# A macaron decoder layer on one core: three more tiles of the second feed-forward in the wide form, and the decay vectors made behind another head

## The chip, the cores and the metric

The kernel runs on one core of a Trainium2 chip. The metric is device time in microseconds (us) for one execution, the median of several runs. The core has a matrix engine (PE, whose weight loads are shown apart as PEld), a vector engine (DVE), a scalar engine (ACT), GpSimd (POOL) and a sync engine (SP) that here only issues DMAs. Each engine works through its own list of instructions strictly in order, and engines wait for each other by semaphores. Matmul results land in PSUM, which has eight banks of 128 partitions x 512 fp32 values; everything else lies in SBUF.

## The reference

One decoder layer over 512 tokens of width 1024, all fp32:

```python
f = swiglu(rms_norm(h, ffn1_norm_pre), ffn1_w_gate, ffn1_w_up, ffn1_w_down)
h = h + 0.5 * rms_norm(f, ffn1_norm_post)
u = rms_norm(h, mix_norm_pre)
q, k, v, xr, yr, gl = split(u @ w_in)          # 12 heads of 128; 1024; 1024; 2 x 1024
attn = 3 groups of 4 heads, dilated sliding windows, merged by log-sum-exp
xc = width-4 causal convolution of xr
log_a = -8 * sigmoid(gate_a) * softplus(-a_param)      # RG-LRU, a recurrence over time
rec = scan(exp(log_a), ...) * gelu(yr)
merged = sigmoid(gl)[0] * (attn @ w_attn) + sigmoid(gl)[1] * (rec @ w_rec)
h = h + rms_norm(merged @ w_out, mix_norm_post)
f = swiglu(rms_norm(h, ffn2_norm_pre), ffn2_w_gate, ffn2_w_up, ffn2_w_down)
h = h + 0.5 * rms_norm(f, ffn2_norm_post)
```

where `swiglu(x) = (silu(x @ w_gate) * (x @ w_up)) @ w_down` with a hidden width of 2816, which is 22 tiles of 128.

## The kernel before, in words

**fp32 products from three.** An fp32 operand is split into a high part (ACT copies it into the matrix engine's fp32r type, line 303) and a low part (DVE subtracts, line 304). A product is then three matmuls: high x high, high x low, low x high. Every weight goes through such a split on the chip: SP fetches 512 KB into one of four `raw` slots (line 243), ACT and DVE split it into one of four `w8` tiles, and only when the low part is done is the `raw` slot free for the next fetch.

**Seven products instead of eight.** Most pairs of weight tiles go through one level of Strassen's method in Winograd's form. For hidden tile `f` of a feed-forward, the weights of up (`u0`, `u1`) and gate (`g0`, `g1`) are fetched, four sums of them are made on DVE, and all seven forms are split (`w_forms`, lines 685 to 703: four additions at lines 692, 693, 694 and 697, then three splits of 1024 columns and one of 512). The products p1 to p7, each over four blocks of k, then make 128 x 512 results of gate and up. The forms of tile f+1 are made while tile f is on PE.

There are two ways to do the seven products.

- `seven_on` (the narrow form, matmuls at lines 730 to 732): each result is 256 columns wide, each block of k takes three matmuls of 256 columns, 84 matmuls in all. Four half banks of PSUM are used. Results on the way are copied by ACT alone (line 744, four copies of 256 columns); DVE adds at lines 970 and 975 and makes the final product of gate and up in two halves at line 980; silu runs in two halves on ACT (lines 984 and 971).
- `seven_wide` (the wide form, matmuls at lines 782 and 783): high and low part of the activations stand side by side, so that high x high and high x low are one matmul of 512 columns, and low x high one of 256. That is 56 matmuls, into five whole banks. A result lies in two halves of its bank that must be added: `move` copies 512 columns from bank to bank on ACT (line 788, three of them), `fold` copies one half out on ACT (line 794) and adds the other on DVE (line 796), and `sum_of` is two additions on DVE (lines 804 and 806). Silu is one ACT instruction of 512 columns (line 988), and the product of gate and up is one of DVE (line 989).

In both forms PE adds p6 onto the bank from which ACT has just copied p1, and p4 onto a bank that ACT has just filled, so PE waits for ACT at such places if ACT is late.

**The second feed-forward** (called `ffn(2, ...)`) handles hidden tiles 0 to 2 in the standard way, tiles 3 and 4 by a third variant of the seven products, and tiles 5 to 21 by `seven_on`, except for the tiles named in `WIDE[2]`, which take `seven_wide`. The choice is one test in `prod`, `if f in WIDE[n]`. The down-projection of finished groups of four tiles (`FF_PARTS`) is done in four steps, one behind each of tiles 4 to 19 (`down7`, matmuls at lines 1065 to 1067): step 0 behind tiles 4, 8, 12, 16, step 1 behind 5, 9, 13, 17, step 2 behind 6, 10, 14, 18 and step 3 behind 7, 11, 15, 19. Its weights are prepared in `d_forms` (sums at lines 1007, 1012, 1016, 1021): steps 0 and 2 take two `raw` fetches, steps 1 and 3 one. ACT seeds PSUM with earlier sums (line 1053) and copies the results out (line 1070). The last tile of a group, step 3, also ends with the sums and splits of the activations (lines 925 to 935), which run during the tile behind it. Behind tile 19 the sums of the four parts are merged on DVE (lines 1080 to 1087).

**Attention** (`attend`, once for each of four heads) is interleaved with the q and k projections of the next head, all in the wide form, and behind the last head with the four pairs of branch-gate tiles, wide too, whose results go through `gate` (two Sigmoids on ACT, lines 1521 and 1522). Attention uses Exp on ACT.

**The decay vectors** (`decay`, lines 1208 to 1229) turn `a_param` into 4 and -8 times its softplus, two tiles of 128 x 8, by a series: 30 small DVE instructions in one chain and one Exp on ACT (line 1216). They are first read in the recurrence (lines 1669 and 1671), far behind attention. The call stands in the loop over heads. `tc.issue_after(x)` orders what is traced in it behind the instruction `x` on x's engine: here the ACT work behind the last Exp of that head (`state["exp"]`, line 1465) and the DVE work behind the last subtraction of that head (`state["low"]`, line 1505).

**What sets the order.** A scheduler orders each engine's list before the run: program order is the priority, `tc.high_priority(offset=...)` moves instructions ahead by as many places (weights 100, copies out of PSUM 200), and an instruction is issued once its inputs are there by the scheduler's own reckoning. The instructions of `decay` have no raised priority; they stand in program order where the call stands.

Of the kernel before, what the change touches and what calls it, by code (L numbers as in the profile page):

```python
# [20 lines left out]
NF = 22  # L21
FF_PARTS = ((0, 4), (4, 8), (8, 12), (12, 16), (16, 22))
NSTD = {1: 6, 2: 3}
WIDE = {1: (), 2: (9, 13, 17)}

SEVEN = range(4)
STEPS_AT = {1: ((6, 7, 7, 8), range(9, 13), range(13, 17), range(17, 21)),
# [2 lines left out]
NH = 4  # L30
# [154 lines left out]
def hybrid_layer(ctx: ExitStack, tc: tile.TileContext, xT: bass.AP, xN: bass.AP, wst: bass.AP,  # L185
# [126 lines left out]
    def tmp(name):  # L312
        return tpool.tile([P, T], F32, name=name, tag="t")
# [550 lines left out]
    def ffn(n, x, r, forms_x, apool, pss):  # L864
# [96 lines left out]
        def prod(f, w):  # L961
            g, u = tmp("g"), tmp("u")
            if f in WIDE[n]:
                seven_wide(t, w, *([x[:, h] for h in HALVES] for x in (g, u)), then=forms_left)
# [243 lines left out]
    def decay(pool):  # L1208

        o, w = SMALL["ap"]  # L1210
        av = sm[:, o:o + w]
        na, ex, zz = (s8(n, pool) for n in ("na", "ex", "zz"))
        po, sp8 = decays
        DVE.tensor_scalar(na, av, -1.0, None, op0=ALU.mult)
        DVE.tensor_tensor(ex, av, na, op=ALU.min)
        ACT.activation(ex, ex, AF.Exp)
        DVE.tensor_scalar(zz, ex, 2.0, None, op0=ALU.add)
        DVE.reciprocal(zz, zz)
        DVE.tensor_mul(zz, zz, ex)
        DVE.tensor_mul(ex, zz, zz)  # L1220
        DVE.memset(po, 1.0 / 19.0)
        for i in (17, 15, 13, 11, 9, 7, 5, 3, 1):
            DVE.tensor_mul(po, po, ex)
            DVE.tensor_scalar(po, po, 1.0 / i, None, op0=ALU.add)
        DVE.tensor_mul(po, po, zz)
        DVE.tensor_scalar(na, na, 0.0, None, op0=ALU.max)
        DVE.scalar_tensor_tensor(po, po, 2.0, na, op0=ALU.mult, op1=ALU.add)
        DVE.tensor_scalar(sp8, po, -8.0, None, op0=ALU.mult)
        DVE.tensor_scalar(po, po, 4.0, None, op0=ALU.mult)

    with ExitStack() as mx:
# [143 lines left out]
        def qk(hd):  # L1375

            q, k = [], []
            for g in range(NG):
                w = pair_of(("pair",) + pairs[hd][g])
                tq, tk = (apool.tile([P, T], F32, name="qk", tag="qk", bufs=QKB) for _ in range(2))  # L1380
                if g == 0:
                    seven_wide(t, w, *([nat(x)[:, 2 * i:2 * i + 2] for i in range(2)] for x in (tq, tk)),
                               seen=lambda ap: ap.rearrange("q (p b r) -> q p b r", p=2, b=4))
                else:
                    seven_wide(t, w, *([x[:, h] for h in HALVES] for x in (tq, tk)))
                q.append(tq)
                k.append(tk)
            cs = slice(hd * P, (hd + 1) * P)
            return q, k, [vals[g][:, :, cs] for g in range(NG)]
# [116 lines left out]

        for hd in range(NH):
            attend(hd, qkvs.pop(hd))
            if hd == 1:
                with tc.issue_after(state["exp"]), tc.issue_after(state["low"]):  # L1510
                    decay(apool)
            if hd + 1 < NH:
                qkvs[hd + 1] = qk(hd + 1)
# [378 lines left out]
```

## Time and profile before

| what | value |
|---|---|
| median of 3 runs | 1207.54 us (1207.19 to 1207.65) |
| the profiled execution: its own time | 1207.33 us |
| its span in the trace | 1205.6 us |
| busy PE / PEld / DVE / ACT | 1197.3 / 1065.1 / 1038.8 / 836.1 us |
| granted clock of PE | 0.999 |
| PE MATMUL, lines 782 (big and rb operands) | x452 and x152, mean 397 ns |
| PE MATMUL, lines 730, 731, 732 (big operands) | x788 each, mean 283 ns |
| ACT_TABLE_LOAD, all lines | 1283 ns each |

The profile gives each engine's busy time, the chain of work that ended last, and groups of instructions by line. Matmuls are pipelined: a matmul shows a longer time than the distance to the next, so rates are read here from the length of a stretch over its count. A tile of the second feed-forward is bounded by the first matmul of its seven products and that of the next tile's. The seven products of tile 8 begin at 967.52 us from the span's start, those of tile 9 at 983.06, 10 at 998.41, 11 at 1011.59, 12 at 1027.40, 13 at 1042.94, 14 at 1058.29, 15 at 1071.11, 16 at 1086.80, 17 at 1102.34, 18 at 1117.69, 19 at 1130.51 and 20 at 1146.04.

### The profile page before, as it was taken

Reading aid. Unit: us, or ns where it says so; the run is one execution under the profiler, and the core shown is the slowest. Engines: PE = TensorE matmul, PEld = TensorE weight load, DVE = VectorE, ACT = ScalarE, POOL = GpSimd, SP = SyncE. Lnnn points to the kernel's source line nnn. Section 1 sums busy time; section 2 is a strip of 40 time slices with the busy share of each in tenths; the row PEclk is TensorE's granted clock in tenths of the full one; section 3 lists DMA queues with packets and bytes.
Section 4 is the critical chain, followed back from the end, with each engine's and each line's share of the span. In section 5 each row is a group of like instructions: output and inputs, shape, how many; then the busy total and the mean of one; then the engine's idle time right before and its main releaser. Section 6 shows DMA issues by size and latency. Waiting matters only on the chain.

```text
span 1205.6 us, 18733 instructions
## 1 busy us (share of the span) xinstructions
PE 1197.3 (99%) x7138; PEld 1065.1 (88%) x7138; DVE 1038.8 (86%) x1641; ACT 836.1 (69%) x1453; POOL 26.1 (2%) x51
## 2 busy tenths in 40 slices
PE   9999999999999999999999999999999999999997
PEld 8899999999888889888888888888899989898996
DVE  7999888989689999999868899874798888889974
ACT  6566787887566676767736988734566687878763
POOL 0000000000011000000000000000100000000000
PEclk9999999999999999999999999999999999999999
DMA  7224343434725233222323433235443433333441
GB/s 267 88 94 133 125 140 108 138 112 153 248 101 164 71 97 97 88 79 88 114 63 121 167 117 102 80 113 189 144 141 105 123 123 123 123 125 122 140 175 71
DMA packets 45819, 149.77 MB, mean 124 GB/s; under 512 B 5152, under 2 KB 8608, under 8 KB 45728
## 3 DMA queue, kind: packets, MB, share of 16 engines
q1 hardware_dynamic: 38160, 131.09, 33.3%
q0 software_dynamic: 7280, 17.30, 4.3%
q8 instruction: 56, 0.92, 0.3%
q14 instruction: 35, 0.29, 0.1%
q10 hardware_dynamic: 288, 0.17, 0.0%
HBM read 138.06 MB, written 6.29 MB: 120 GB/s over the span
## 4 chain that ended last, share of the span: by engine, by line
PE 96%; DVE 2%; ACT 1%; DMA 0%; issue 0%; DVEq 0%; ACTq 0%
PE acc L782 11%; PE acc L730 9%; PE acc L732 9%; PE acc L731 9%; PE acc L316 7%; PE acc L318 7%; PE acc L317 7%; PE acc L783 6%; PE aux L1065 4%; PE aux L1066 4%; PE aux L1067 4%; PE acc L434 2%; PE acc L432 2%; PE acc L433 2%; PE aux L434 1%; PE aux L432 1%
## 5 line engine op out<-in xcount | busy, mean ns | idle before, releaser
L304 DVE TENSOR_TENSOR w<-raw,w 128x1024 fp32r<-128x1024 f32 (+1 forms) x272 | 296.9, 1100 | 33.0 <-ACT w L303 31.7
L303 ACT ACTIVATE w<-raw 128x1024 fp32r<-128x1024 f32 (+1 forms) x272 | 259.1, 958 | 86.6 <-PE acc L318 48.7
L730 PE MATMUL acc<-big,w 128*128 128x256 f32 x788 | 223.0, 283 | 0.1
L732 PE MATMUL acc<-big,w 128*128 128x256 f32 x788 | 223.0, 283 | 0.0
L731 PE MATMUL acc<-big,w 128*128 128x256 f32 x788 | 223.0, 283 | 0.0
L782 PE MATMUL acc<-big,w 128*128 128x512 f32 x452 | 161.5, 397 | 0.0
L730 PEld LDWEIGHTS acc<-big,w 128*128 128x128 f32 x788 | 151.0, 192 | 1.5 <-ACT acc L744 0.3
L731 PEld LDWEIGHTS acc<-big,w 128*128 128x128 f32 x788 | 151.0, 192 | 1.3
L732 PEld LDWEIGHTS acc<-big,w 128*128 128x128 f32 x788 | 151.0, 192 | 0.0
L783 PE MATMUL acc<-big,w 128*128 128x256 f32 x452 | 127.4, 282 | 0.0
L782 PEld LDWEIGHTS acc<-big,w 128*128 128x128 f32 x452 | 84.9, 188 | 19.3 <-issue 0.2
L1065 PE MATMUL aux<-w,xf 128*128 128x512 f32 x224 | 87.5, 391 | 0.0
L1066 PE MATMUL aux<-w,xf 128*128 128x512 f32 x224 | 87.5, 391 | 0.0
L1067 PE MATMUL aux<-w,xf 128*128 128x512 f32 x224 | 87.1, 389 | 0.0
L783 PEld LDWEIGHTS acc<-big,w 128*128 128x128 f32 x452 | 85.3, 189 | 0.3
L304 DVE TENSOR_TENSOR w<-s,w 128x1024 fp32r<-128x1024 f32 x51 | 62.3, 1222 | 1.3 <-ACT w L303 1.1
L303 ACT ACTIVATE w<-s 128x1024 fp32r<-128x1024 f32 x51 | 53.9, 1057 | 8.2 <-PE acc L732 4.9
L316 PE MATMUL acc<-xf,w 128*128 128x512 f32 (+1 forms) x168 | 59.1, 353 | 0.0
L317 PE MATMUL acc<-xf,w 128*128 128x512 f32 (+1 forms) x168 | 58.6, 349 | 0.0
L318 PE MATMUL acc<-xf,w 128*128 128x512 f32 (+1 forms) x168 | 58.5, 349 | 0.0
L782 PE MATMUL acc<-rb,w 128*128 128x512 f32 x152 | 55.4, 397 | 0.0
L1067 PEld LDWEIGHTS aux<-w,xf 128*128 128x128 f32 x224 | 42.1, 188 | 9.0
(463 smaller groups left out, 2913.5 us busy)
## 6 DMA issues: line engine op xcount, KB each, us to landing
raw<-in_w SPq DMA_DIRECT2D x232, 512.0 KB, 3.6
big<-xf POOLq DMA_DIRECT2D x6, 512.0 KB, 3.3
gains<-in_rows POOLq DMA_DIRECT2D x5, 512.0 KB, 5.3
h<-in_x SPq DMA_DIRECT2D x8, 256.0 KB, 5.0
h<-in_xn POOLq DMA_DIRECT2D x4, 512.0 KB, 6.5
kept_m<-h POOLq DMA_DIRECT2D x4, 512.0 KB, 2.9
vals<-in_w SPq DMA_DIRECT2D x4, 512.0 KB, 6.3
h<-kept_m POOLq DMA_DIRECT2D x4, 512.0 KB, 5.9
```

The source lines that it names most:

```text
L303: state["split"] = ACT.activation(dh, src, AF.Copy).ins
L304: state["low"] = DVE.tensor_sub(dl, src, dh.bitcast(F32)).ins
L316: PE.matmul(ps, wh, xh, start=first, stop=False)
L317: PE.matmul(ps, wh, xl, start=False, stop=False)
L318: PE.matmul(ps, wl, xh, start=False, stop=last)
L730: PE.matmul(ps, wh, xh, start=start and k == 0, stop=False, skip_group_check=True)
L731: PE.matmul(ps, wh, xl, start=False, stop=False, skip_group_check=True)
L732: state["product"] = PE.matmul(ps, wl, xh, start=False, stop=k == 3, skip_group_check=True).ins
L782: PE.matmul(part, wh, at(BOTH, k), start=start and k == 0, stop=False, skip_group_check=True)
L783: last = PE.matmul(cross, wl, at(0, k), start=False, stop=k == 3, skip_group_check=True)
L1065: PE.matmul(ps, xh, wh, start=first and j == 0, stop=False, skip_group_check=True)
L1067: PE.matmul(ps, xl, wh, start=False, stop=j == 1, skip_group_check=True)
```

## The change

`WIDE[2]` names tiles 7, 9, 11, 13, 15 and 17 instead of 9, 13 and 17, so tiles 7, 11 and 15 go through `seven_wide` instead of `seven_on`. The call of `decay` stands behind head 3, the last one, instead of head 1; the two `issue_after` then refer to head 3's Exp and subtraction. No other line differs.

```diff
 NSTD = {1: 6, 2: 3}
-WIDE = {1: (), 2: (9, 13, 17)}
+WIDE = {1: (), 2: (7, 9, 11, 13, 15, 17)}
...
         for hd in range(NH):
             attend(hd, qkvs.pop(hd))
-            if hd == 1:
+            if hd == NH - 1:
                 with tc.issue_after(state["exp"]), tc.issue_after(state["low"]):
                     decay(apool)
             if hd + 1 < NH:
```

## The prediction

> **What bounds the kernel now.** The page first: its span, its busiest engine, and the engines' shares of the chain of waits.
>
> ```profile
> span 1205.6 us, 18733 instructions
> PE 1197.3 (99%) x7138; PEld 1065.1 (88%) x7138; DVE 1038.8 (86%) x1641; ACT 836.1 (69%) x1453; POOL 26.1 (2%) x51
> PE 96%; DVE 2%; ACT 1%; DMA 0%; issue 0%; DVEq 0%; ACTq 0%
> ```
>
> The reader is to see that PE sets the time nearly alone. What the change can win is the difference in PE's own rate between two forms of a tile plus some of the moments at which PE stands still, and the whole span shows only 1205.6 - 1197.3 = 8.3 us of idle PE, its head and tail included (short stalls besides can hide under matmul ends). Matmuls overlap, so a rate is a stretch over its count. Tile 8 is narrow, tile 9 wide; these are the rows of their seven products alone (the counts hold one or two neighbours):
>
> ```profile
> 967.52:977.60 10.08, 10.08 (x86) 10.07 (x85) 8.63 (x14) 8.35 (x15) 0.00 (x0) 1.00 0.51 158
> 983.06:992.94 9.88, 9.88 (x57) 8.56 (x56) 8.23 (x16) 7.34 (x14) 0.00 (x0) 1.00 0.46 159
> ```
>
> The columns are length, then busy time and count of PE, PEld, DVE, ACT and POOL. 84 matmuls take 10.08 us and 56 take 9.88: a third fewer matmuls, but only 0.20 us, because two of three become one of twice the columns. Next, the stretches from one tile's first matmul to the next tile's, with the down-projection step between them: tiles 9, 10, 11, 14, 15, 16, 18, 19.
>
> ```profile
> 983.06:998.41 15.35, 15.35 (x81) 13.07 (x80) 13.41 (x22) 12.51 (x23) 0.00 (x0) 1.00 0.30 104
> 998.41:1011.59 13.18, 13.08 (x97) 12.39 (x96) 12.08 (x17) 9.60 (x18) 0.00 (x0) 1.00 0.48 160
> 1011.59:1027.40 15.81, 15.78 (x109) 14.62 (x108) 13.65 (x20) 12.47 (x23) 0.00 (x0) 1.00 0.41 134
> 1058.29:1071.11 12.82, 12.82 (x97) 12.33 (x96) 12.11 (x17) 9.84 (x19) 0.00 (x0) 1.00 0.49 164
> 1071.11:1086.80 15.69, 15.69 (x109) 14.64 (x108) 13.52 (x20) 12.34 (x23) 0.00 (x0) 1.00 0.44 137
> 1086.80:1102.34 15.54, 15.54 (x109) 14.58 (x108) 13.83 (x18) 13.44 (x24) 0.00 (x0) 1.00 0.34 101
> 1117.69:1130.51 12.82, 12.82 (x97) 12.33 (x96) 12.82 (x18) 10.36 (x19) 0.00 (x0) 1.00 0.49 169
> 1130.51:1146.04 15.53, 15.53 (x109) 14.58 (x108) 15.53 (x19) 11.47 (x21) 0.54 (x1) 1.00 0.41 132
> ```
>
> An undisturbed narrow tile with a long step takes 15.54 (tile 16), one with a short step 12.82 (tile 14). Tile 10, behind wide tile 9, takes 13.18 and loses 0.36; tile 11 loses 0.27; tile 15, second behind wide tile 13, loses 0.15; tiles 14 and 18, right behind wide tiles, lose nothing. So the stage holds some 0.8 us of stalls, and they stand behind wide tiles. DVE is full in tiles 18 and 19 (12.82 of 12.82, 15.53 of 15.53), and still PE doesn't wait there.
>
> Why tile 10 loses time is in the chain of waits, start and length:
>
> ```profile
> 998.82 0.70 DVE w L304
> 999.53 5.14 DMA raw<-in_w
> 1004.70 0.81 ACT w L303
> ...
> 1006.98 0.28 ACT acc L744
> 1007.30 0.39 PE acc L730
> ```
>
> DVE's last subtraction for a weight frees a raw slot, the fetch that waited for it lands 5.14 us later, ACT splits that weight, and the copy for which PE waits stands behind the split in ACT's list. A wide tile loads DVE and by this path makes the next tile late.
>
> **The change part by part.** *Three wide tiles, the rate.* 3 x (10.08 - 9.88) = -0.60 us, on PE, so on the path. [...]
>
> *Their work on DVE and ACT.* Of the groups of DVE in the stretch of tiles 13 to 16 (one wide, three narrow), the first of each size:
>
> ```profile
> L975 DVE TENSOR_TENSOR u<-acc,c 128x256 f32<-128x256 f32 x3 | 1.3, 420 | 0.0
> L796 DVE TENSOR_TENSOR c<-acc,c 128x256 f32<-128x256 f32 x2 | 0.8, 425 | 1.1 <-ACT c L794 1.1
> L804 DVE TENSOR_TENSOR c<-acc,c 128x256 f32<-128x256 f32 x2 | 0.8, 419 | 0.0
> L989 DVE SCALAR_TENSOR_TENSOR tt<-g,u 128x512 f32<-128x512 f32 x1 | 0.7, 687 | 0.0
> ```
>
> A narrow tile has four of 128x256 at 0.42 us (lines 970, 975, 980 twice) = 1.68; a wide one has eight of 0.42 (796 four times, 804 and 806 twice each) and one of 0.69 = 4.05. So 2.37 us more of DVE for each converted tile. The room: tiles 15 and 16 together have (15.69 - 13.52) + (15.54 - 13.83) = 3.88 us of DVE idle, tiles 11 and 12 alike. So it fits, and I cost DVE's time itself at nothing; what hides it is that idle time and the weights' lead, bounded under the rivals. ACT had 13.44 of 15.54 in its fullest tile.
>
> What I do cost is the path seen in tile 10. The three existing wide tiles lost 0.36, 0 and 0 in the tile behind. Tiles 7, 11 and 15 have the same shape of neighbours: their step (3) needs one raw fetch as step 1 does, the tile behind needs two more. At the mean of 0.12: 3 x 0.12 = **+0.36**; bounds nothing, and each as bad as tiles 10 and 11 together, 3 x 0.63 = +1.9. The losses inside tiles 11 (0.27) and 15 (0.15), now rewritten, may go or grow: 0, bounds -0.42 and +0.6 (in tile 11 the wide form's copy is of 512 columns instead of 256, and something like another 0.3 each).
>
> *Decay leaves head 1.* What the chain has of it where PE stalls among the next head's scores, and the matmul ahead of the stall:
>
> ```profile
> 516.52 0.16 DVE zz L1219
> ...
> 516.88 0.08 DVE ex L1220
> ...
> 517.56 0.08 DVE po L1223
> 517.64 0.35 DVE facc L1414
> 518.03 1.16 PE aux L1433 x8
> ```
>
> ```profile
> 517.44 0.28 PE L783 MATMUL acc<-big,w 128*128 128x256 f32 x1
> ```
>
> All in all 30 DVE instructions spread over 20 us. In the chain they hold 0.08 each (the next one starts that soon, though one alone takes 0.16): three of them, 0.24 us, stand ahead of the subtraction at line 1414 for which PE waits. That goes: **-0.24**; bounds -0.47 (the whole stall: a matmul of 256 columns takes 10.08 / 84 = 0.12, and 518.03 - 517.44 - 0.12 = 0.47) and 0. What is late next is the DVE work between them, line 697, 0.60.
>
> *Decay arrives behind head 3.* DVE has room there:
>
> ```profile
> 589.00:601.00 12.00, 12.00 (x73) 10.65 (x73) 8.06 (x17) 10.00 (x19) 0.00 (x0) 1.00 0.49 160
> 601.00:623.00 22.00, 22.00 (x99) 18.04 (x98) 15.31 (x22) 6.19 (x8) 0.00 (x0) 1.00 0.32 104
> ```
>
> Some 4 us idle ahead of 601, 6.7 behind; 30 x 0.08 = 2.4 us fits, cost nothing, and its readers come far behind. No DMA is issued by it and no queue is passed. But ACT is another matter:
>
> ```profile
> 587.56 1.28 ACT L1521 ACT_TABLE_LOAD   x1
> 588.85 0.63 ACT L1521 ACTIVATE facc<-g 128x512 f32<-128x512 f32 x1
> ...
> 591.96 1.06 ACT L303 ACTIVATE w<-raw 128x1024 fp32r<-128x1024 f32 x1
> 592.90 0.60 ACT L788 ACTIVATE acc<-acc 128x512 f32<-128x512 f32 x1
> ...
> 599.11 0.63 ACT L1521 ACTIVATE facc<-g 128x512 f32<-128x512 f32 x1
> ```
>
> ```profile
> 591.38 0.68 DVE L1505 TENSOR_TENSOR attn<-aux,attn 128x512 fp32r<-128x512 f32 x1
> ```
>
> ```profile
> L1216 ACT ACTIVATE ex<-ex x1: 219/219/219, 510.5 to 510.5; 128x8 f32<-128x8 f32 x1
> ```
>
> Attention's Exp and the gate's Sigmoid need different tables: at 587.56 the first Sigmoid brings a load of 1.28 us. Head 3's subtraction (line 1505) starts at 591.38, behind it, so decay's Exp falls behind that load: it needs a load of its own, and the Sigmoid at 599.11 another. 2 x 1.28 + 0.22 (the Exp at head 1 took 219 ns) = 2.8 us more on ACT. Behind the Exp wait the split at line 303, the copy at line 788 and all further copies of that pair of tiles, and PE waits for those.
>
> ```profile
> 594.01 0.40 PE L782 MATMUL acc<-rb,w 128*128 128x512 f32 x1
> ```
>
> The copy at line 788 ends at 593.50, and p6, which adds onto the bank that it fills, starts at 594.01. If load and Exp go in at 593.02, ahead of that copy, it ends at 593.02 + 1.28 + 0.22 + 0.60 = 595.12 and PE loses 1.1 us. If they go behind it, they fill ACT's gaps (0.70 and 1.08 us before the next two copies) and PE loses nothing. I take **+0.5**, between 0 and 1.1. The second load, at 599.11, stands behind that pair's last bank copy; the products behind have 6.19 of 22 us on ACT: nothing.
>
> *Sum:* -0.60 + 0.36 + 0 - 0.24 + 0.5 = **+0.02 us**. Against the profiled execution's 1207.33 that is 1207.35; the median lies 0.2 above it, and I give **1207.4 us**. All lower ends: -0.60 - 0.42 - 0.47 = -1.5, so 1205.8. All upper ends: -0.60 + 1.9 + 0.6 + 1.1 = +3.0, so 1210.3.
>
> **The rivals.**
>
> *Clean win:* DVE hides everything, the old stalls of tiles 11 and 15 and of head 2 go, the Exp finds a gap: all lower ends, 1205.8. For it: in tiles 18 and 19 DVE is full and PE doesn't wait. Against: tiles 10 and 11.
>
> *Two table loads on the path:* both hold ACT while PE waits, 1.1 + 1.28 = 2.4 instead of 0.5: +1.9, 1209.3. For it: decay stands ahead of the last pairs in program order, so a ready Exp goes first. Against: the load at 587.56 cost PE nothing. The Trainium skill, page "ScalarE: Activation LUTs", section "What ACT_TABLE_LOAD costs", makes it worse: 1283 ns and a drain of about 1380 with each switch, estimated 2.66 us each, which would carry this rival to some 1212. The trace has the 1283, but the Sigmoid starts at 588.85, 0.01 us behind the load, so no drain shows.
>
> *DVE becomes the bound (slower):* the place is tiles 17 to 19, where DVE has no idle time, so delay that arrives there stays.
>
> ```profile
> 1125.11 1.22 DVE L304 TENSOR_TENSOR w<-raw,w 128x1024 fp32r<-128x1024 f32 x1
> 1127.51 1.22 DVE L304 TENSOR_TENSOR w<-s,w 128x1024 fp32r<-128x1024 f32 x1
> ```
>
> Tile 19's first weights are ready at 1126.33 and used at 1130.51; the second at 1128.73 and used one product (1.44 us) later, at 1131.95: a lead of 3.2 us. Past 3.2 us of delay PE waits. One converted tile brings 2.37; if the idle time of the tiles between can't be used, because DVE stands there waiting for ACT, two bring 4.7 and PE loses 1.5, with the raw fetches late all along (+1.9): -0.60 + 1.9 + 1.5 + 0.26 = +3.1, 1210.4. Against: 3.88 us idle right there.
>
> That the change doesn't do what it says I leave out: form and place are each one test in the program.
>
> **How the numbers follow.** Forecast (within about 1.2 of 1207.4) 0.53; clean win 0.15, of which 0.03 over 0.2% faster; table loads 0.15; DVE bound 0.17, of which 0.16 over 0.2% slower. 0.2% is 2.4 us, about what a measurement of this kernel can tell from no change: faster is below 1205.1, slower above 1209.9. So faster 0.03, same 0.81, slower 0.16. The range leaves out most of the DVE rival and the outermost of the win: 1205.9 to 1209.9.
>
> **What would show it.** Tiles 7, 11 and 15 from start to start: 15.35 if the rate is right. Tiles 8, 12 and 16: 15.54 if no path through the raw slots, up to 0.4 more each if so. Table loads at line 1216 and twice at line 1521: the ACT step; a p6 of the last gate pair that waits for line 788: its price. The stall ahead of line 1433's matmuls of head 2 down to some 0.2: decay's leaving. Wrong would be a lead below zero for the weights of tiles 18 to 20, or a different order of the lists elsewhere, which I can't see beforehand.

## The result, and the profile after

| what | value |
|---|---|
| changed kernel, median of 9 runs | 1210.72 us (1209.75 to 1212.06) |
| kernel before, beside it, 9 runs | 1207.41 us (1207.17 to 1208.92) |
| ratio, with 95% interval | 1.0025 (1.0017 to 1.0034) |
| the profiled execution's own time, and its span | 1209.75 us, 1208.0 us |

The changed kernel is 3.3 us slower. The forecast was no change, 1207.4 with a range of 1205.9 to 1209.9, so the measured 1210.72 lies outside it. The profiled execution is the fastest of the nine: against the profiled execution of before it is 1209.75 - 1207.33 = 2.42 us slower, and that difference is taken apart here.

The page of the changed kernel, the same lines as were shown of before:

```profile
span 1208.0 us, 18601 instructions
PE 1198.0 (99%) x7054; PEld 1060.6 (88%) x7054; DVE 1045.9 (87%) x1656; ACT 841.7 (70%) x1461; POOL 26.1 (2%) x51
PE 88%; DVE 6%; ACT 3%; DMA 2%; issue 1%; DVEq 0%; ACTq 0%
```

PE's busy time hardly shows the loss (matmul ends cover short stalls), but its share of the chain fell from 96% to 88%: DVE, ACT and DMA now end waits. DVE is busy for 7.1 us more, as forecast (3 x 2.37).

The second feed-forward by tiles, from each first matmul to the next tile's, tiles 7, 10, 11, 13, 14, 15, 17 and 18 (length, then busy time and count of PE, PEld, DVE, ACT, POOL):

```profile
951.27:966.62 15.35, 15.35 (x82) 13.09 (x81) 11.17 (x18) 10.83 (x19) 0.00 (x0) 1.00 0.30 100
997.58:1011.09 13.51, 13.08 (x98) 12.38 (x96) 12.07 (x17) 9.59 (x18) 0.00 (x0) 1.00 0.46 158
1011.09:1026.86 15.77, 15.47 (x81) 13.01 (x80) 13.55 (x22) 12.69 (x23) 0.00 (x0) 1.00 0.29 101
1042.60:1058.28 15.68, 15.61 (x82) 13.08 (x81) 13.51 (x22) 11.92 (x22) 0.00 (x0) 1.00 0.36 122
1058.28:1072.46 14.18, 13.06 (x97) 12.38 (x96) 12.35 (x17) 10.45 (x20) 0.00 (x0) 1.00 0.32 112
1072.46:1088.35 15.89, 15.65 (x82) 13.07 (x80) 13.53 (x22) 12.69 (x23) 0.00 (x0) 1.00 0.29 101
1103.99:1119.76 15.77, 15.64 (x81) 13.07 (x80) 15.30 (x25) 12.53 (x23) 0.00 (x0) 1.00 0.37 120
1119.76:1132.89 13.13, 13.06 (x97) 12.37 (x96) 13.10 (x18) 11.05 (x20) 0.00 (x0) 1.00 0.39 125
```

An undisturbed tile takes 15.54 (narrow, long step), 15.35 (wide, long step) or 12.82 (narrow, short step). Tile 7 shows the wide form undisturbed. The others lose 0.69 (tile 10), 0.42 (11), 0.33 (13), **1.36 (14)**, 0.54 (15), 0.42 (17) and 0.31 (18); tiles 8, 9, 12 and 16 lose 0.37 together (tile 9 is 0.06 shorter). That is 4.44 where before lost 0.78 (tiles 10, 11 and 15), so 3.66 more, less 0.57 for the rate of three wide tiles: +3.1 us. Ahead of this stage the changed kernel had gained 0.7 (tile 5 begins at 922.91 instead of 923.62), and 3.1 - 0.7 = 2.4 is the difference of the two executions.

Tile 14, the largest loss. First the chain of waits (start, length), then ACT and PE in order of time (start, length, and in brackets the idle time before and what ended it):

```profile
1058.37 2.37 DVE w L304 x2
...
1060.76 4.74 DMA raw<-in_w
```

```profile
1065.58 1.06 ACT L303 ACTIVATE w<-raw 128x1024 fp32r<-128x1024 f32 x1 [1.82 <-DMA raw<-in_w]
1066.55 1.04 ACT L303 ACTIVATE w<-s 128x1024 fp32r<-128x1024 f32 x1
...
1067.76 0.37 ACT L744 ACTIVATE acc<-acc 128x256 f32<-128x256 f32 x1
```

```profile
1068.18 0.39 PE L730 MATMUL acc<-big,w 128*128 128x256 f32 x1 [1.12 <-ACT acc L744]
```

DVE's split frees a raw slot at 1060.74, 2.46 us into the tile. The fetch lands at 1065.50. ACT stood idle for it for 1.82 us, then makes two splits, and only behind them comes the copy out of PSUM for which PE's p4 waits. It is the path that the prediction read in tile 10, 1.3 us deep. These rows say how the loss comes about, not why DVE was late; the experiments were made for that.

### The profile page after: what moved, and what is told of

Its sections match the earlier page's. It is cut to its first block, busy times and chain, and to the rows that moved or that the text cites. A ratio compares the mean times of both kernels' runs of the same rounds, so it can differ in the third digit from the quotient of the medians.

```text
span 1208.0 us, 18601 instructions
## 1 busy us (share of the span) xinstructions
PE 1198.0 (99%) x7054; PEld 1060.6 (88%) x7054; DVE 1045.9 (87%) x1656; ACT 841.7 (70%) x1461; POOL 26.1 (2%) x51
## 4 chain that ended last, share of the span: by engine, by line
PE 88%; DVE 6%; ACT 3%; DMA 2%; issue 1%; DVEq 0%; ACTq 0%
PE acc L782 12%; PE acc L316 7%; PE acc L318 7%; PE acc L317 7%; PE acc L730 7%; PE acc L732 7%; PE acc L731 7%; PE acc L783 6%; PE aux L1065 3%; PE aux L1066 3%; PE aux L1067 3%; DVE w L304 3%; PE acc L434 2%; PE acc L433 2%; PE acc L432 2%; DMA raw<-in_w 2%
## 5 line engine op out<-in xcount | busy, mean ns | idle before, releaser
L730 PE MATMUL acc<-big,w 128*128 128x256 f32 x716 | 203.2, 284 | 1.6 <-ACT acc L744 1.5
L732 PE MATMUL acc<-big,w 128*128 128x256 f32 x716 | 202.6, 283 | 0.0
L731 PE MATMUL acc<-big,w 128*128 128x256 f32 x716 | 202.6, 283 | 0.0
L782 PE MATMUL acc<-big,w 128*128 128x512 f32 x524 | 186.8, 397 | 0.0
L783 PE MATMUL acc<-big,w 128*128 128x256 f32 x524 | 147.2, 281 | 0.0
L730 PEld LDWEIGHTS acc<-big,w 128*128 128x128 f32 x716 | 137.1, 192 | 3.6 <-ACT acc L744 2.2
L731 PEld LDWEIGHTS acc<-big,w 128*128 128x128 f32 x716 | 137.2, 192 | 1.2
L732 PEld LDWEIGHTS acc<-big,w 128*128 128x128 f32 x716 | 137.2, 192 | 0.0
L782 PEld LDWEIGHTS acc<-big,w 128*128 128x128 f32 x524 | 98.4, 188 | 22.7
L783 PEld LDWEIGHTS acc<-big,w 128*128 128x128 f32 x524 | 98.8, 189 | 0.4
L788 ACT ACTIVATE acc<-acc 128x512 f32<-128x512 f32 x75 | 44.2, 589 | 13.2 <-PE acc L783 11.7
```

What stands on the lines that cost most here:

```text
L730: PE.matmul(ps, wh, xh, start=start and k == 0, stop=False, skip_group_check=True)
L731: PE.matmul(ps, wh, xl, start=False, stop=False, skip_group_check=True)
L732: state["product"] = PE.matmul(ps, wl, xh, start=False, stop=k == 3, skip_group_check=True).ins
L782: PE.matmul(part, wh, at(BOTH, k), start=start and k == 0, stop=False, skip_group_check=True)
L783: last = PE.matmul(cross, wl, at(0, k), start=False, stop=k == 3, skip_group_check=True)
```

## The experiments

All stand beside runs of the kernel before on the same chip (medians 1207.29 to 1207.47). The last column is the difference of the two medians; the intervals of the ratios are some 1 us to either side.

| run | what it is | median, us | ratio to before (95%) | us over before |
|---|---|---|---|---|
| changed kernel | | 1210.72 | 1.0025 (1.0017 to 1.0034) | +3.3 |
| e1_wide_only | six wide tiles, decay at head 1 | 1210.54 | 1.0027 (1.0017 to 1.0038) | +3.3 |
| e2_decay_only | three wide tiles, decay at head 3 | 1206.31 | 0.9992 (0.9984 to 1.0001) | -1.0 |
| e3_dve_load | e2 and DVE's extra work in narrow tiles | 1206.06 | 0.9989 (0.9980 to 0.9998) | -1.2 |
| e4_act_load | e2 and ACT's | 1206.49 | 0.9992 (0.9984 to 1.0001) | -0.8 |
| e7_both_loads | e2 and both | 1206.68 | 0.9993 (0.9984 to 1.0002) | -0.8 |
| e6_even_tiles | six other wide tiles | 1206.49 | 0.9995 (0.9987 to 1.0004) | -1.0 |
| e8_tile_11 | e2 and tile 11 wide | 1207.21 | 0.9998 (0.9989 to 1.0006) | -0.3 |
| e5_product_first | changed, product earlier | 1207.90 | 1.0008 (0.9999 to 1.0017) | +0.4 |
| e13_sum_held | changed, one sum later | 1208.01 | 1.0004 (0.9995 to 1.0013) | +0.6 |
| e9_copy_first | changed, copy ahead of splits | 1208.12 | 1.0006 (0.9997 to 1.0015) | +0.7 |
| e10_both_orders | e5 and e9 | 1207.93 | 1.0005 (0.9996 to 1.0014) | +0.5 |
| e11_four_even | four wide tiles without a late product | 1206.64 | 0.9993 (0.9985 to 1.0002) | -0.8 |
| e12_decay_head2 | before, decay at head 2 | 1207.16 | 0.9999 (0.9991 to 1.0008) | -0.2 |

The first theory was **A**: the amount of work that the wide form brings to DVE makes raw slots late. Rivals: **B**, ACT's longer copies stall PE directly; **C**, the form's own waits in its five banks.

### The two parts alone

```diff
 # e1_wide_only: decay at hd == 1, and
+WIDE = {1: (), 2: (7, 9, 11, 13, 15, 17)}
 # e2_decay_only: WIDE as before, and
+            if hd == NH - 1:
```

> One part alone: tiles 7, 9, 11, 13, 15 and 17 wide, decay at head 1 as before. Theory A (DVE's extra work delays the release of raw slots, the fetch lands late, and ACT's splits, late too, stand ahead of the copies for which PE waits): the second feed-forward loses about 3.1 us as in the changed kernel, and 0.7 to 0.9 us that decay's move won are not there: +3.1 to +4 us against before, 1210.5 to 1211.5. If the loss came from decay's move instead (a changed order of the lists), this one is within 0.5 us of before.

> The other part alone: decay behind head 3, tiles 9, 13 and 17 wide as before. From the two traces: 0.7 to 0.9 us less than before, 1206.5 to 1206.8, with tiles 5 to 21 of the second feed-forward within 0.3 us of before's. If decay's move upset the order of the lists in the second feed-forward, more than before.

The wide tiles carry the loss, +3.3. Decay's move looks like a gain, -1.0, a little more than expected, with an interval that just reaches no change. Their sum is +2.3 and the changed kernel showed +3.3; the intervals cover that, and the two profiled executions differ by 2.4.

### The loads without the form

```diff
+                def more(src, i):
+                    if n == 2 and f in (7, 11, 15):
+                        free = u[:, lo]
+                        with tc.high_priority(offset=EVAC):
+                            for _ in range((2, 2, 1, 1, 1)[i]):          # e3, e7
+                                DVE.tensor_add(free, src, src)
+                            for _ in range((1, 1, 1, 1, 0)[i]):          # e4, e7
+                                ACT.activation(free, src, AF.Copy)
```

`more` is called behind each of the copies c5 and c6 and behind the additions at lines 970 and 975; what it writes is overwritten later.

> As decay alone, and in the narrow tiles 7, 11 and 15 seven additions of 128x256 more on DVE, right behind the copies out of PSUM, results unused: 7 x 0.35 = 2.45 us more of DVE in each, about what the wide form brings (2.37). No wide tile is added. Theory A: PE loses in these tiles and the tile behind, as in the changed kernel: 3 to 4.5 us over decay alone. Rival B (ACT's longer copies and moves of the wide form stall PE directly): no more than 0.5 us over decay alone. Rival C (the form's own waits in its five banks): the same as B.

> As decay alone, and in the narrow tiles 7, 11 and 15 four copies of 128x256 more on ACT, results unused: 4 x 0.38 = 1.5 us more of ACT in each, about what the wide form brings (1.6). Theory A: within 0.5 us of decay alone. Rival B: PE loses 3 us or so over decay alone. Rival C: within 0.3 us of decay alone.

> Decay alone with both loads in the narrow tiles 7, 11 and 15: seven additions of 128x256 on DVE and four copies of 128x256 on ACT, results unused, so that both engines have as much as in the wide form at once. Theory D (the place of the last product in the list, which this doesn't touch): within 0.5 us of decay alone, 1205.8 to 1206.8. Theory A in the form that is left (only both loads together stall PE): 2 us or more over decay alone, 1208.3 and up.

None of them cost anything that shows. In e3_dve_load DVE was busy for 1046.8 us against 1039.1 without the load, 7.7 more (the changed kernel: 7.1). In e4_act_load ACT was busy for 842.6 us against 839.5 (the changed kernel: 841.7). Tile 11 of e3_dve_load, the group of the added instructions and then the tile:

```profile
L975 DVE TENSOR_TENSOR u<-c 128x256 f32<-128x256 f32 x7 | 2.9, 421 | 0.5 <-ACT c L744 0.4
```

```profile
1009.95:1025.64 15.69, 15.69 (x110) 14.64 (x109) 15.16 (x25) 11.89 (x22) 0.00 (x0) 1.00 0.29 101
```

DVE is busy for 15.16 of 15.69 us, 2.9 of them added, and the tile is as long as tile 15 was before. **A falls, and B as an amount of work**: on either engine or on both it is hidden, as the prediction had costed it. That PE can still wait for one of ACT's copies because of its place in the list is another matter, and it does so below.

### Other tiles, and one tile

```diff
+WIDE = {1: (), 2: (6, 8, 10, 12, 14, 16)}   # e6_even_tiles, decay at the last head
+WIDE = {1: (), 2: (9, 11, 13, 17)}          # e8_tile_11, decay at the last head
```

A new theory, **D**, came from the two orders of DVE's list. Tiles 7, 11 and 15 are the last of their groups of four. A group's last product of gate and up is needed at once, for the sums and splits of the activations (lines 925 to 935). In the narrow form it stands in two halves (line 980) at the tile's end. In the wide form it is one instruction (line 989; neither line has a raised priority) and stands behind the next tile's weight sums and splits. DVE around the end of tile 11, first before (the tile runs from 1011.59 to 1027.40), then in the changed kernel (1011.09 to 1026.86):

```profile
1026.29 0.42 DVE L980 SCALAR_TENSOR_TENSOR tt<-g,u 128x256 f32<-128x256 f32 x1
1026.62 1.22 DVE L304 TENSOR_TENSOR w<-raw,w 128x1024 fp32r<-128x1024 f32 x1
```

```profile
1026.12 1.83 DVE L304 TENSOR_TENSOR w<-raw,w 128x1024 fp32r<-128x1024 f32 x2
1027.87 1.22 DVE L1007 TENSOR_TENSOR sum<-raw 128x1024 f32<-128x1024 f32 x1
1029.01 0.69 DVE L989 SCALAR_TENSOR_TENSOR tt<-g,u 128x512 f32<-128x512 f32 x1
```

The second half of the product, or the product as a whole, comes 14.7 us from the tile's start before and 17.9 in the changed kernel.

> Six wide tiles, every second one, as in the changed kernel, but 6, 8, 10, 12, 14 and 16 instead of 7 to 17; none of these is the last of a group of four. Decay at the last head. Theory D (the last of a group): within 1 us of decay alone, 1205.5 to 1207.3. Theory A (the amount of work, with no narrow pair between to make up for it): as slow as the changed kernel, 1209.5 to 1211.

> One converted tile alone: 9, 11, 13 and 17 wide, decay at the last head. In the changed kernel tile 11 and the three tiles behind it lost 0.56, 0.21, 0.34 and 1.38 us. Theory D: one late product is enough, so tiles 11 to 14 lose about 2.3 us, less 0.2 of rate, over decay alone: 1208 to 1208.6. If the loss needs every second tile wide (work that piles up from tile to tile): under 0.8 us over decay alone, below 1207.1.

Six wide tiles in other places cost nothing against decay alone, so the form itself and its spacing are not the cause (C falls as well). Tile 8 of e6_even_tiles, wide and undisturbed, with ACT fuller than in any tile of before that was shown (14.43 us; 13.44 there):

```profile
966.12:981.47 15.35, 15.35 (x82) 13.08 (x80) 13.90 (x23) 14.43 (x25) 0.00 (x0) 1.00 0.33 102
```

Tile 11 alone brought 0.9 over decay alone (0.7 by the last column), less than the 1.7 to 2.3 that D had for it and about at the 0.8 that bounded the other theory, so the time of this run doesn't decide between the two. (The expectations add up PE's waits where this text goes by tile lengths, so tile 11's 0.56 there is 0.42 here.) Its DVE list in tile 13 is turned over in the same way as in the changed kernel, as D has it, and the fetch for tile 14 is as late (2.60 us into the tile). But that fetch took 3.57 us there instead of 4.74, and tile 14 lost only 0.32.

### The order of the lists

DVE in tile 13 of the changed kernel, in order of time; and the same places in e2_decay_only, where tile 13 is wide too but tile 11 is not:

```profile
1049.96 1.23 DVE L1016 TENSOR_TENSOR raw<-raw 128x1024 f32<-128x1024 f32 x1 [1.21 <-DMA raw<-in_w]
...
1051.44 1.22 DVE L304 TENSOR_TENSOR w<-sum,w 128x1024 fp32r<-128x1024 f32 x1
...
1059.50 1.83 DVE L304 TENSOR_TENSOR w<-raw,w 128x1024 fp32r<-128x1024 f32 x2
```

```profile
1048.34 1.23 DVE L304 TENSOR_TENSOR w<-sum,w 128x1024 fp32r<-128x1024 f32 x1 [0.52 <-ACT w L303]
...
1056.61 1.83 DVE L304 TENSOR_TENSOR w<-raw,w 128x1024 fp32r<-128x1024 f32 x2
1058.35 1.22 DVE L1016 TENSOR_TENSOR raw<-raw 128x1024 f32<-128x1024 f32 x1
```

Tile 13 begins at 1042.60 in the one and 1042.00 in the other, tile 14 at 1058.28 and 1057.35. The sum at line 1016, for the down-projection of tile 14, stands last in e2_decay_only and in the middle of tile 13 in the changed kernel. There DVE stands still for 1.21 us until its fetch has landed, works on it for 1.23, and all splits behind it are late; the pair of splits that frees the raw slots starts 1.22 us into tile 14 instead of 0.74 us ahead of it. Three kernels change only the order of the changed kernel's lists; their instructions are the same. (e5_product_first moves the product of every wide tile, and that of tiles 3 and 4, which share the line; in e9_copy_first DVE's list shifts a little too in tiles 10 and 14.)

```diff
 # e5_product_first
+            def put(dst, v):
+                with tc.high_priority(offset=EVAC): DVE.scalar_tensor_tensor(dst, v(g), -1.0, v(u), op0=ALU.mult, op1=ALU.mult)
+            with tc.high_priority(offset=EVAC): ACT.activation(g, g, AF.Silu)
+            into(f, put)
 # e13_sum_held: last_w is the last split of the next tile's weights (w_forms)
+                    with tc.issue_after(state["last_w"]) if n == 2 else nullcontext(): DVE.tensor_add(u0, u0, u1)
 # e9_copy_first: the weights of tiles 11 and 15 are traced behind prod, and
+                    if n == 2 and ev[1] in (11, 15):
+                        edges.enter_context(tc.issue_after(state["kept"]))
```

> The changed kernel with the same instructions in another order: silu and the product of gate and up of a wide tile (lines 988 to 993) get the priority of the copies out of PSUM, so that they stand in their engines' lists at the tile's end and no longer behind the next tile's weight sums and splits. Theory D (tiles 7, 11 and 15 are the last of their groups; their late product pushes the sums and splits of the activations into tiles 9, 13 and 17, turns the order of DVE's list over there, so that DVE waits for fetches and releases raw slots late): the losses of tiles 13 and 14 (0.34 and 1.38) and of tile 17 (0.40) go, 1.5 to 2.5 us less than the changed kernel, 1208.2 to 1209.2. Theory A (the amount of DVE work): within 0.5 us of the changed kernel, 1210.2 to 1211.2.

> The changed kernel with one thing held back on DVE: the sum of the down weights at line 1016 stands behind the last split of the next tile's weights, as it does in the kernel before, and not in the middle of tiles 13 and 17, where DVE waited 1.21 us for its fetch. The product at line 989 stays as late as in the changed kernel. If that one place in the list is what makes the raw slots late for tile 14: its fetch is issued some 1.1 to 1.5 us after the tile's start instead of 2.48, its stall of 1.38 us goes or falls below 0.4, and the time is 0.8 to 1.4 us less than the changed kernel, 1209.3 to 1209.9; the stalls of tiles 10 to 13 stay. If the late activations' forms alone make it late (they still stand at the start of tile 13): the fetch stays beyond 2 us and the time within 0.4 us of the changed kernel.

> The changed kernel with one thing reordered on ACT in tiles 10 and 14: the splits of the next tile's weights stand behind the last copy out of PSUM (line 744) instead of ahead of it; the instructions are the same. Over the runs so far PE's stall ahead of p4 in these two tiles is the landing of the first of the three fetches issued there, less 5.95 us from the tile's start (landed at 7.22, 7.16, 6.17 and 5.62 us: 1.28, 1.21, 0.23 and no stall). Theory D with that path (late release, fetch, split on ACT, copy behind it): the stalls of 0.69 and 1.38 us go whatever the fetch takes, 1.5 to 2.1 us less than the changed kernel, 1208.5 to 1209.3. If PE waited for something else there (a bank, DVE): no change, 1210.3 to 1211.3. If the later splits make the weights of tiles 11 and 15 late: a stall at the start of those tiles in place of the other.

> The changed kernel with both reorderings: product first, and copy first in tiles 10 and 14. Product first left 1.38 us of stall in tile 10 and none in 14, and stood at 1207.9. Theory D: the 1.38 goes, 1206.3 to 1207.0, about as fast as decay alone. If the paths only hand the loss on: 1207.5 and up.

**e5_product_first** takes 2.8 us off the changed kernel, a little more than expected. The product of tile 11, at 17.9 us from that tile's start in the changed kernel, now comes at 11.5 (first row, tile 11 from 1011.57):

```profile
1023.07 0.68 DVE L989 SCALAR_TENSOR_TENSOR tt<-g,u 128x512 f32<-128x512 f32 x1
...
1059.54 1.22 DVE L1016 TENSOR_TENSOR raw<-raw 128x1024 f32<-128x1024 f32 x1
```

Line 1016 is back in tile 14 (second row), though this edit doesn't touch it: the late product had turned the list over two tiles further on. Tiles 13 and 14 are undisturbed:

```profile
1042.81:1058.16 15.35, 15.35 (x82) 13.09 (x80) 14.02 (x23) 12.19 (x23) 0.00 (x0) 1.00 0.27 89
1058.16:1070.98 12.82, 12.82 (x98) 12.33 (x96) 12.79 (x18) 10.46 (x20) 0.00 (x0) 1.00 0.47 166
```

**e13_sum_held** leaves the product late and moves line 1016 alone. DVE's splits and sum, and tile 14 (from 1058.59):

```profile
1057.86 1.83 DVE L304 TENSOR_TENSOR w<-raw,w 128x1024 fp32r<-128x1024 f32 x2 [0.16 <-ACT w L303]
1059.60 1.22 DVE L1016 TENSOR_TENSOR raw<-raw 128x1024 f32<-128x1024 f32 x1
```

```profile
1058.59:1071.41 12.82, 12.82 (x97) 12.33 (x96) 12.11 (x17) 9.85 (x19) 0.00 (x0) 1.00 0.46 165
```

The fetch for which ACT's split waits is issued 1.12 us into tile 14 again, the losses of tiles 14 and 18 (1.36 and 0.31) are gone, and the others are much as they were (tile 11 loses 0.59, tile 15 0.31). The time fell by 2.7 us, more than the 0.8 to 1.4 expected and more than the 1.67 of these two tiles. The profiled executions differ by 1.74, but that of the changed kernel was its fastest and this one the median of its eleven; the fastest of each differ by 2.8. Where the other 1 us lies isn't shown. By the medians, putting this one sum back in its place, in tiles 13 and 17, takes back most of the 3.3 us.

**e9_copy_first** leaves DVE as late as it is and takes ACT's splits out of the way. ACT in tile 14 (from 1057.42; the copy is line 750 here, the split 309), and tiles 10 and 14:

```profile
1064.87 0.38 ACT L750 ACTIVATE acc<-acc 128x256 f32<-128x256 f32 x1
1065.18 1.04 ACT L309 ACTIVATE w<-raw 128x1024 fp32r<-128x1024 f32 x1
```

```profile
997.48:1010.30 12.82, 12.82 (x97) 12.33 (x96) 12.01 (x17) 10.14 (x19) 0.00 (x0) 1.00 0.49 166
...
1057.42:1070.30 12.88, 12.88 (x98) 12.39 (x96) 12.26 (x17) 10.92 (x20) 0.00 (x0) 1.00 0.36 123
```

The fetch is issued 2.73 us into tile 14, as late as ever, and PE loses 0.06. The time is 2.6 us below the changed kernel, again a little more than expected. The link in the middle, a fetch ahead of splits ahead of a copy in ACT's list, is shown by this.

**e10_both_orders** missed the expectation of D; the time is that of either edit alone, as the sentence on paths that hand the loss on had it. Tiles 10 and 14 are undisturbed, but tiles 8, 12 and 15 to 19 lose 0.06 to 0.50 each, 1.9 together; in tiles 12, 16 and 17 it is again ACT's copies that PE waits for. So not all of the loss is found: all four reordered kernels lie 1.4 to 1.7 us above decay alone by the last column, where three more wide tiles should lie 0.6 below it, and about 2 us of loss stay in each.

How the fetch enters is seen by putting the executions beside each other. The fetch for which ACT's first split of the next tile's weights waits is the first of the three that the expectations speak of; in e12_decay_head2 and e5_product_first another one goes out 0.6 us ahead of it. From the chain of waits of e1_wide_only, e8_tile_11 and e12_decay_head2 (tile 14, from 1059.34, 1057.84 and 1057.82) and of e5_product_first (tile 10, from 997.38), in this order:

```profile
1061.90 4.59 DMA raw<-in_w
```

```profile
1060.44 3.57 DMA raw<-in_w
```

```profile
1058.93 5.45 DMA raw<-in_w
```

```profile
998.87 5.79 DMA raw<-in_w
```

They land 7.15, 6.17, 6.56 and 7.28 us into the tile, and p4 starts 1.21, 0.23, 0.56 and 1.28 late, counted from when the matmul ahead of it lets it; in the changed kernel 7.22 and 1.28. Each is the landing less 5.95, within 0.05. The changed kernel's rows say why: p4 is due 72 x 0.12 = 8.64 after the tile's start, and it starts 1068.18 - 1065.50 = 2.68 behind the landing, which leaves 5.96. Past that point a late release and a long fetch count alike: in e12_decay_head2 the fetch was issued as early as before (1.11 us into the tile), and PE lost by its length alone.

### A better version, and decay's place

```diff
+WIDE = {1: (), 2: (6, 8, 12, 16)}           # e11_four_even, decay at the last head
 # e12_decay_head2: WIDE as before, and
+            if hd == 2:
```

> A version meant to beat both: decay at the last head, and 6, 8, 12 and 16 wide. In the run with the even tiles these four were wide without a stall, while 10 and 14, whose fetches come three at a time, lost 0.30 each. Against decay alone: one wide tile more, 0.20 less, the 0.1 each in tiles 11 and 15 gone: 1205.8 to 1206.3. If even these make the tiles behind late: 1206.8 and up.

> The kernel before with decay at head 2 instead of head 1; the tiles of the second feed-forward as before. If what the move won is that its 30 small DVE instructions no longer stand among the scores of a next head: no gain at head 2, where head 3's scores follow, 1207.0 to 1207.8, with stalls of 0.4 to 1 us in head 3. If the gain came from leaving head 1 alone: as decay alone, 1206.3.

e11_four_even missed by 0.3: its tiles 5 to 18 have no stall at all, but tile 20 loses 0.6, as it does in e6_even_tiles. Why is open. The versions with decay at the last head and no late product (e2, e3, e4, e6, e7, e11) all lie 0.8 to 1.2 us below the kernel before, with intervals that mostly just reach 1; among them nothing can be told apart. Decay alone is the simplest.

At head 2 decay's chain stands among head 3's scores, as at head 1 among head 2's. The chain of waits ahead of PE's stall there:

```profile
555.04 0.07 DVE ex L1220
...
555.72 0.08 DVE po L1223
555.79 0.35 DVE facc L1414
...
556.18 0.82 PE aux L1433 x5
```

PE stands for 0.44 us, as it did for 0.47 in head 2 before, and attention as a whole takes 256.96 us (before 256.76). So the gain is that of leaving the scores, not of leaving head 1. By the times alone (-0.2 against -1.0, each with some 1 us to either side) this wouldn't be shown.

## Why the prediction was wrong

**The rate** (-0.60): right. Tile 7 takes 15.35, a narrow one 15.54; 3 x 0.19 = 0.57.

**DVE's time costed at nothing**: right as an amount, by e3_dve_load and e7_both_loads.

**The step that failed** is the one behind it: "Tiles 7, 11 and 15 have the same shape of neighbours", so that each would lose what tiles 9, 13 and 17 lose behind them, 3 x 0.12 = +0.36, at most +1.9. Measured, in the profiled execution, +3.12 in all tiles but 11 and 15 (0.75 of it inside tiles 13 and 17, below). The neighbours' shape was compared by the number of raw fetches; that these three are the last of their groups, whose product the activations' forms wait for, was in the kernel's text (lines 925 to 935) and was not used. The form moves that product from the tile's end to 2 us into the next tile, and the list that follows from it puts line 1016 ahead of ready splits: 1.67 us in tiles 14 and 18. This is what the prediction named as a sign of being wrong, "a different order of the lists elsewhere", and gave no price.

The 0.12 had a weak ground besides: "A wide tile loads DVE and by this path makes the next tile late" was read from one execution. Tile 10's fetch was issued 1.12 us into the tile there, as early as in executions without a stall, and took 5.14 us. In the six other profiled executions with tile 9 wide and tile 7 narrow (e2, e3, e4, e7, e8 and e12) it took 4.1 to 4.6, and tile 10 lost nothing. In the six with tile 7 wide (the changed kernel, e1, e5, e9, e10 and e13) it took 5.1 to 5.8. In the changed kernel, issued at 1.11 us again, it took 5.49 and tile 10 lost 0.33 more; e9_copy_first shows that PE loses it by the same path. What makes this fetch longer isn't shown.

**Inside tiles 11 and 15** (0, between -0.42 and +0.6): +0.54, within the bounds. p6, which adds onto the bank that the copy at line 788 fills, waits for that copy, and the copy stands behind a split. Tiles 13 and 17 have the same wait now, 0.33 and 0.42, which no term held. With the product earlier (e5_product_first) tiles 11, 13 and 15 lose nothing and tile 17 still 0.49; with line 1016 held back alone (e13_sum_held) the four lose 0.28 to 0.59 each. So these waits go with the late product more than with line 1016. ACT and PE in tile 11:

```profile
1012.77 1.05 ACT L303 ACTIVATE w<-raw 128x1024 fp32r<-128x1024 f32 x1
1013.72 0.59 ACT L788 ACTIVATE acc<-acc 128x512 f32<-128x512 f32 x1
```

```profile
1014.35 0.49 PE L782 MATMUL acc<-tx,w 128*128 128x512 f32 x1 [0.29 <-ACT acc L788]
```

**Decay leaves** (-0.24) **and arrives** (+0.5), +0.26 together: measured -1.0 (e2_decay_only). This error hides part of the other one: the wide tiles alone, forecast at -0.24 and at most +1.9, cost 3.3. In attention, from its first wide matmul to the last, before took 256.76 us and e1_wide_only 257.50, the kernels with decay at head 3 between 255.70 and 256.42. The whole stall of 0.47 went, not three instructions' 0.24 of it, and one of 0.38 at 543.54 in the next head with it, whose cause is open. The arrival is mechanically as forecast, a load at line 1216 and two at line 1521:

```profile
581.94 1.28 ACT L1521 ACT_TABLE_LOAD   x1
...
587.41 1.28 ACT L1216 ACT_TABLE_LOAD   x1
588.71 0.21 ACT L1216 ACTIVATE ex<-ex 128x8 f32<-128x8 f32 x1
...
590.39 1.28 ACT L1521 ACT_TABLE_LOAD   x1
```

But no wait of PE reaches 0.1 us from 582 to 600: the loads fell where the copies had slack. Head 3's last subtraction, expected at 591.38, came at 585.42, and decay's Exp with it ahead of the second Sigmoid.

The Trainium skill, page "ScalarE: Activation LUTs", section "What ACT_TABLE_LOAD costs", adds a drain of about 1380 ns to each switch. Here the load starts 0.02 us behind the copy ahead of it and the Exp, at 588.71, 0.02 us behind the load, so no drain shows here either.

**The rivals.** The slower one gave 1210.4 at 0.17, and that this is near the measured 1210.72 is in good part luck. Half of its mechanism happened: raw fetches were late because "DVE stands there waiting", but for a fetch and not for ACT, and in tiles 14 and 18 and not all along. Its place was wrong. It lay at tiles 17 to 19 and hung on a lead of 3.2 us running out; tile 19 takes 15.54 in the changed kernel, so no lead ran out. What decided is not an average of DVE's room but one wait in its list. The chance of 0.81 for no change rested on DVE's idle time, and by e3_dve_load that was not the limit.

Open: why the order turns over where it does is the scheduler's reckoning, which was seen only by its results; the 2 us of loss that stay in the reordered kernels; what makes the fetch of tile 10 longer; and tile 20's loss in e6 and e11.

## What to carry to other kernels

When a change lengthens a tile's work on an engine with room, don't ask first whether the room suffices, but which of the moved instructions somebody waits for next, and where it will stand in the list: here 2.4 us of added work a tile cost nothing, and one product that came 3 us later in a list (6 later than where e5_product_first put it) cost most of 3.3. Where a scheduler orders the lists, an edit in one tile can reorder another two tiles on; compare the lists around each place where an instruction waits for a transfer with ready work behind it. And read the slack of such a chain from the profile (here a landing at 5.95 us into the tile): a fetch whose length varies by 2 us eats it by itself.

## What the runs showed of the hardware

512 KB fetches into the same slots took very different times. Over the whole of the changed kernel the median is 3.5 us, and the fetch for line 1016, with one other beside it for 1 us, took 3.45. The fetch for which ACT waits in tiles 10 and 14, issued 1.1 to 2.7 us into the tile with two or three others soon beside it, took 3.57 to 5.79 in the executions above.

```profile
raw<-in_w SPq DMA_DIRECT2D x232, 512.0 KB, 3.5
```

```profile
1046.38 3.45 DMA raw<-in_w
```

The Trainium skill, page "DMA: Bandwidth & Descriptors", section "Anatomy of one DMA — SWDGE (gpsimd) path", fits 2.0 us and the bytes over 436 GB/s for DMAs that GpSimd issues; estimated from that page 512 KB take 3.2 us. These fetches are issued by SP, so it is a comparison only: the 3.45 us is near it, and the 5.79, with others beside it, 2.6 us above.
